# Splits of weights pinned in program order: the first of block 2 behind the experts' last copies, four of the feed-forward behind the layer norm

## The chip, the cores and the metric

One core of a Trainium2 chip. The metric is device time in microseconds (us) of one execution, as the median of several runs. The engines are PE (matrix products), ACT (ScalarE), DVE (VectorE), POOL (GpSimd) and SP (SyncE, which issues the DMAs here); each works through its own queue of instructions in order, and semaphores between them carry what one needs of another.

## The reference

Two blocks of a network, in fp32, for 256 tokens of width 1024. Block 1 is a mixer (attention and short convolution) and a mixture of experts; block 2 is a second mixer (attention and a gated MLP), a layer norm, a SwiGLU feed-forward of hidden width 2816, and a last layer norm:

```python
def first_block(x, ...):
    h = rms_norm(x, norm_mix_g[l])
    ...
    x = x + merged @ w_out[l]
    h2 = rms_norm(x, norm_ffn_g[l]).reshape(B * S, D)
    y = hierarchical_moe(h2, w_router_group[l], b_router_group[l], w_router_expert[l],
                         b_router_expert[l], w_gate_e[l], w_up_e[l], w_down_e[l])
    x = x + y.reshape(B, S, D)

def hierarchical_moe(...):
    for g in range(N_GROUPS):
        sl = slice(g * EXPERTS_PER_GROUP, (g + 1) * EXPERTS_PER_GROUP)
        act = jax.nn.silu(jnp.einsum('nd,edf->nef', h, w_gate[sl])) * jnp.einsum('nd,edf->nef', h, w_up[sl])
        act = act * combine[:, g, :, None]
        y = y + jnp.einsum('nef,efd->nd', act, w_down[sl])

def second_block(x, ...):
    mix = hybrid_mixer(x, w_in[l], ...)
    x = layer_norm(DEEPNORM_ALPHA * x + mix, ln1_g[l], ln1_b[l])
    ffn = swiglu_ffn(x, w_gate[l], w_up[l], w_down[l])
    x = layer_norm(DEEPNORM_ALPHA * x + ffn, ln2_g[l], ln2_b[l])

def swiglu_ffn(x, w_gate, w_up, w_down):
    return (jax.nn.silu(x @ w_gate) * (x @ w_up)) @ w_down
```

## The kernel before

All weights come from HBM as tiles of 128 x 2048 fp32 values (1 MB), which `Feed` loads through one ring of buffers: a buffer that is given back starts the DMA of the next tile in a fixed list, on SP's queue (L79). Products of weights with activations that need fp32 precision are made in three PE passes: each half tile of 128 x 1024 is split into a high part `whi` and a low part `wlo`, and the activations likewise (`xh` and `xl`). A **split** is two instructions, in `hi_lo` (L265 to 267): ACT copies the high part (L266), DVE subtracts it from the weight (L267). The class `Split` keeps the list of half tiles and makes splits ahead of their use: `ahead(n)` makes all up to the n-th, `get` hands one out and keeps `lead` splits in front of PE. Both write their instructions where the program calls them; under `manual_schedule` with `in_order` the engines keep the order of the program, but outside such a stretch, and where no instruction is tied down, a list scheduler sets the order of each engine.

The stages that matter here, in order of time:

- **The last expert group** (`group`, from L810). Eight rounds of gate and up products `pc_t<-w,xg` (L814), each followed by 12 small filler products on an otherwise idle bank (`warm`, L239), which use no result. Then `h = silu(gate) * up` on ACT and DVE (L843, L844), two transposes on PE (L848), the copy `hT` (L849), and the down products `pc_t<-w,hT` with four down tiles, their sums copied to `y` by ACT (L872, L867) and DVE, and PE's products of `y` with the scatter matrix (L854).
- **Block 2's first projection** (from L1108). `W.ahead(1)` splits the first half tile; then block 2's input, in `acc`, is made into high and low pieces of 256 columns (L266 and L267, the tile `x`), then come the second and the third split, and PE multiplies the pieces with the halves (L279).
- **The layer norm's stage** (from L1194). The end of the output projection is added to `xres` by DVE (L1180), with statistics (L1171 to 1176: `bst`, `mv`, `ve`), the reciprocal root `rs` on POOL (L257), the shift `mr` (L1197), the normalised rows `xn` on ACT (L1200), their transposes on PE (L1207), high and low pieces of them (`x`), and the first feed-forward products over two slices' gate and up weights together (L1237, L1240).
- **The feed-forward** (from L1268). 22 slices of 128 hidden columns. Slice f has a gate half and an up half (`fgu`), each multiplied with the pieces by `dense_wide` (L294, L295), whose two sums per bank DVE adds up (`gated`, L1272 to 1281: `fs`, `fu`), ACT applies silu to, DVE multiplies; `hi_lo` makes the slice's `fh` and `fl`. Every two slices the down projection's half tiles (`fdn`) are multiplied with these (L279, `pa_t<-whi,fh`). Each `W.get` in `hidden` asks for splits `lead` ahead; `W.lead` is set to 2 at the start of this stage and grows by one with each `get` (`W.grow`) up to the number of buffers.

Which split stands where, before: the scheduler sets block 2's first split on ACT and DVE ahead of `h` of the last group, and four splits of the feed-forward among DVE's and ACT's steps of the layer norm, as the listings below show.

Of the kernel before, what the change touches and what calls it, by code (L numbers as in the profile page):

```python
# [8 lines left out]
F32 = mybir.dt.float32  # L9
F32R = mybir.dt.float32r  # L10
I32 = mybir.dt.int32
BF16 = mybir.dt.bfloat16
AF = mybir.ActivationFunctionType
ALU = mybir.AluOpType
AX = mybir.AxisListType
PSUM = bass.MemoryType.PSUM

P = 128
D = 1024
KD = D // P  # L20
S = 256
# [13 lines left out]
WBUF = 3  # L35
WBUF2 = 9
# [90 lines left out]
def fused_blocks(ctx: ExitStack, tc: tile.TileContext, a, out):  # L127
# [4 lines left out]
    tt = nc.vector.tensor_tensor  # L132
    ts = nc.vector.tensor_scalar
    stt = nc.vector.scalar_tensor_tensor
    red = nc.vector.tensor_reduce
    act = nc.scalar.activation
# [7 lines left out]
    units_a, units_b, order = [], [], []  # L144
# [120 lines left out]
    def hi_lo(hi, lo, src):  # L265
        act(hi, src, AF.Copy)  # L266
        tt(out=lo, in0=src, in1=hi.bitcast(F32), op=ALU.subtract)  # L267

    def gained(hi, lo, src, g):
        act(hi, src, AF.Copy, scale=g)  # L270
# [664 lines left out]
    wes, wp = pool("w_b", bufs=WBUF2, side="left")  # L935
    xes, xp = pool("x_b", side="left")
    ees, ep = pool("blk2", side="right")
    W = Split(feed, wp, units_b, hi_lo, WBUF2, WBUF + 2)
    x_hl = xp.tile([P, 2, KD, S], F32R, name="x2")
    xh, xl = x_hl[:, 0], x_hl[:, 1]  # L940
    mh = xp.tile([P, KD, S], F32R, name="mh2")
# [164 lines left out]

    with tc.manual_schedule(engines=in_order):
        W.ahead(1)  # L1108
        for k in range(2):
            hi_lo(xh[:, k, :], xl[:, k, :], acc[0][:, k, :])  # L1110
        W.ahead(2)
        for k in range(2, KD, 2):
            hi_lo(xh[:, k:k + 2, :], xl[:, k:k + 2, :], acc[k // 2])
        W.ahead(3)
        for k in range(0, KD, 2):
            act(x2T[k // 4][:, k % 4:k % 4 + 2, :], acc[k // 2], AF.Copy)
        b2["z2"] = proj_tok(W, "z2", xh, xl, then([], [(x2_tok, 0, 0)], [(x2_tok, 0, 1)], [(x2_tok, 1, 0)]), bank_c)
# [68 lines left out]
    def scaled(o, t, cols, bias):  # L1186
        return stt(out=o, in0=xn[:, t, cols], scalar=ln[t][1], in1=bias[:, cols], op0=ALU.mult, op1=ALU.add)  # L1187

    tok = [slice(t * P, (t + 1) * P) for t in range(NT)]
    half = [slice(0, 512), slice(512, D)]  # L1190
    quarter = [slice(i * 256, (i + 1) * 256) for i in range(4)]
    with tc.manual_schedule(engines=in_order):
        for c in range(2):
            attn_rows(0, (3,), (c,))  # L1194
            stats(0, c, add_mix)
        shift = small(fp, 1, "mr")
        stt(out=shift, in0=ln[0][0], scalar=-1.0, in1=ln[0][1], op0=ALU.mult, op1=ALU.mult)  # L1197
        attn_rows(1, (0, 1), (0, 1))
        for cols in half:
            act(xn[:, 0, cols], xres[:, 0, cols], AF.Identity, scale=ln[0][1], bias=shift)  # L1200
        attn_rows(1, (2, 3), (0,))
        stats(1, 0, add_mix)

        def turned(src, t, k, z):

            for i in range(2):
                tr(z[:, k % 4 + i, :], src[:, t, (k + i) * P:(k + i + 1) * P], ident)  # L1207

        def in_chunks(z):
            return z.rearrange("p (k s) -> p k s", k=4)  # L1210

        z0 = [in_chunks(bank_c()) for _ in range(2)]
        for j in range(4):
            turned(xn, 0, 2 * j, z0[j // 2])
        attn_rows(1, (2, 3), (1,))
        ws = [[W.get("fgu", 4 + 2 * f + i) for i in range(2)] for f in range(2)]
        zs = [[two_parts(new()) for _ in range(2)] for new in (bank, bank_c)]

        def split3(t, j, src):
            ks = slice(2 * j, 2 * j + 2)  # L1220
            hi_lo(xh[:, ks, tok[t]], xl[:, ks, tok[t]], src)

        def part0(j):

            x3 = fp.tile([P, 2, P], F32, tag="x3", name="x3", bufs=2)
            for i in range(2):
                kc = 2 * j + i
                act(x3[:, i, :], z0[j // 2][:, kc % 4, :], AF.Identity, scale=V("ln1_g", kc), bias=V("ln1_b", kc))
            split3(0, j, x3)

        def first_hidden(t, j):

            for kc in (2 * j, 2 * j + 1):
                f = slice(kc * P, (kc + 1) * P)
                for w, z in zip(ws, zs):
                    for (hi, lo), z_ in zip(w, z):
                        mm(z_[:, :, tok[t]], hi[:, f], both(x_hl, kc, tok[t]), start=kc == 0 and t == 0, stop=False,  # L1237
                           skip_group_check=True)
                        if t:
                            mm(z_[:, 0, :], lo[:, f], xh[:, kc, :], start=False, stop=kc == KD - 1,  # L1240
                               skip_group_check=True)

        ln1 = feed.get("ln1")
        g1, b1 = ln1[:, 0:D], ln1[:, D:2 * D]
        part0(0)
        stats(1, 1, lambda t, c, o: (add_mix(t, c, o), part0(1)))
        part0(2)
        centred(1, half[0], g1)
        part0(3)
        for j in range(4):  # L1250
            first_hidden(0, j)
        z1 = [in_chunks(bank_c()) for _ in range(2)]

        def part1(j):
            scaled(xres[:, 1, quarter[j]], 1, quarter[j], b1)
            turned(xres, 1, 2 * j, z1[j // 2])

        part1(0)
        for j in range(4):
            if j < 3:  # L1260
                part1(j + 1)
            split3(1, j, z1[j // 2][:, 2 * (j % 2):2 * (j % 2) + 2, :])
            if j == 0:
                centred(1, half[1], g1)
            first_hidden(1, j)
        W.lead = 2


    acc = None
    held = {}  # L1270

    def gated(f, zg, zu):  # L1272
        s, u = [fp.tile([P, S], F32, tag=n, name=n, bufs=2) for n in ("fs", "fu")]
        red(out=s, in_=zg.rearrange("p b s -> p s b"), axis=AX.X, op=ALU.add)
        act(s, s, AF.Silu)
        red(out=u, in_=zu.rearrange("p b s -> p s b"), axis=AX.X, op=ALU.add)
        tt(out=s, in0=u, in1=s, op=ALU.mult)
        if f % 2 == 0:
            held[f // 2] = [fp.tile([P, 2, S], F32R, tag=n, name=n, bufs=2) for n in ("fh", "fl")]
        h_, l_ = held[f // 2]  # L1280
        hi_lo(h_[:, f % 2, :], l_[:, f % 2, :], s)

    def hidden(f):
        z = []
        for _ in range(2):
            z.append(two_parts(bank_c()))
            dense_wide(*W.get("fgu"), KD, x_hl, z[-1])
        gated(f, *z)

    for i in range(12):  # L1290
        if i < 11:
            for f in (2 * i, 2 * i + 1):
                if i:
                    hidden(f)
                else:
                    gated(f, *zs[f])
        if i in (1, 2):

            tc.keep_in_program_order(tt(out=xres[:, 0, :], in0=(xn if i == 1 else xres)[:, 0, :],
                                        in1=g1 if i == 1 else b1, op=ALU.mult if i == 1 else ALU.add))  # L1300
        if i == 2:
            feed.done(ln1)
        if 0 < i < 10:
            acc = acc or four_banks()
            rows_proj(W, "fdn", acc, *held.pop(i - 1), 0, i == 1, False)
# [110 lines left out]
```

## Time and profile before

| what | value |
|---|---|
| time, median of 3 runs | 708.74 us (708.24 to 709.82) |
| the profiled execution's own time | 707.57 us |
| its span in the profile | 705.8 us |
| mean clock granted to PE, share of full speed | 0.985 |
| PE busy | 656.4 us (93%) |
| DVE busy | 367.4 us (52%), of it 186.2 us in 151 low parts (L267) |
| ACT busy | 270.3 us (38%), of it 158.2 us in 151 high parts (L266) |
| POOL busy | 46.0 us (7%) |
| moved by DMA | 185.62 MB, mean 263 GB/s |

[...] In a timeline each row is a run of equal instructions on one engine: its start, the time from the start of the first to the end of the last, the line, the operation, and in brackets how long the engine was idle before and what released it. Neighbouring rows can overlap by some 0.1 us, since an instruction begins while the one ahead of it drains. A span of the profile is shorter than the time of the same execution, here by 1.77 us.

### The profile page before, as it was taken

Reading aid. Unit: us, or ns where it says so; the run is one execution under the profiler, and the core shown is the slowest. Engines: PE = TensorE matmul, PEld = TensorE weight load, DVE = VectorE, ACT = ScalarE, POOL = GpSimd, SP = SyncE. Lnnn points to the kernel's source line nnn. Section 1 sums busy time; section 2 is a strip of 40 time slices with the busy share of each in tenths; the row PEclk is TensorE's granted clock in tenths of the full one; section 3 lists DMA queues with packets and bytes.
Section 4 is the critical chain, followed back from the end, with each engine's and each line's share of the span. In section 5 each row is a group of like instructions: output and inputs, shape, how many; then the busy total and the mean of one; then the engine's idle time right before and its main releaser. Section 6 shows DMA issues by size and latency. Waiting matters only on the chain. (4 is left out here: it accounts for less than half of the span.)

```text
span 705.8 us, 10415 instructions
## 1 busy us (share of the span) xinstructions
PE 656.4 (93%) x4249; PEld 513.5 (73%) x4249; DVE 367.4 (52%) x578; ACT 270.3 (38%) x413; POOL 46.0 (7%) x60
## 2 busy tenths in 40 slices
PE   7999999999999898987787899999799999999995
PEld 6888999999955444434344588877588888888884
DVE  6667565555531202111000189867659766666646
ACT  6567644444300000000000295576535444444410
POOL 2222100000100000000000006101100000000001
PEclk9999999999999999999899799999999999999998
DMA  8983379738979999999999665742317755555001
GB/s 336 408 347 120 126 294 353 253 123 335 410 289 414 419 420 418 420 420 417 414 418 418 258 245 201 276 173 76 122 43 266 279 192 202 195 179 178 1 1 59
DMA packets 27558, 185.62 MB, mean 263 GB/s; under 512 B 3312, under 2 KB 3824, under 8 KB 5872
## 3 DMA queue, kind: packets, MB, share of 16 engines
q1 hardware_dynamic: 27504, 184.89, 67.5%
q8 instruction: 35, 0.57, 0.3%
q14 instruction: 19, 0.16, 0.1%
HBM read 183.83 MB, written 1.05 MB: 262 GB/s over the span
## 5 line engine op out<-in xcount | busy, mean ns | idle before, releaser
L267 DVE TENSOR_TENSOR wlo<-w,whi 128x1024 fp32r<-128x1024 f32 (+1 forms) x151 | 186.2, 1240 | 107.6 <-ACT whi L266 107.2
L266 ACT ACTIVATE whi<-w 128x1024 fp32r<-128x1024 f32 (+1 forms) x151 | 158.2, 1056 | 194.7 <-PE pa_t L279 59.8
L294 PE MATMUL pc_t<-x,whi 128*128 128x512 f32 x320 | 113.5, 399 | 0.0
L295 PE MATMUL pc_t<-x,wlo 128*128 128x256 f32 x320 | 89.8, 281 | 0.0
L294 PEld LDWEIGHTS pc_t<-x,whi 128*128 128x128 f32 x320 | 60.1, 188 | 14.8
L814 PE MATMUL pc_t<-w,xg 128*32 128x512 f32 x512 | 60.8, 615 | 5.0 <-PEq L886 5.0
L295 PEld LDWEIGHTS pc_t<-x,wlo 128*128 128x128 f32 x320 | 60.4, 189 | 0.4
L764 DVE TENSOR_TENSOR xg<-pc_t,vec 128x512 f32<-128x512 f32 (+2 forms) x18 | 11.4, 633 | 80.4 <-PE pc_t L763 80.4
L814 PEld LDWEIGHTS pc_t<-w,xg 128*32 128x32 f32 x512 | 15.5, 112 | 38.5 <-issue 34.8
L279 PE MATMUL pa_t<-whi,x 128*128 128x512 f32 x128 | 41.9, 397 | 0.0
L854 PEld LDWEIGHTS pa_t<-st,y 128*128 128x128 f32 x128 | 23.0, 189 | 21.9 <-DVE y L870 12.5
L854 PE MATMUL pa_t<-st,y 128*128 128x256 f32 x128 | 31.9, 392 | 6.3 <-DVE y L870 6.2
L814 PE MATMUL pc_t<-w,hT 128*32 128x512 f32 (+1 forms) x272 | 32.5, 593 | 4.1 <-ACT hT L849 4.1
L288 PE MATMUL pc_t<-xh,wlo 128*128 128x256 f32 x128 | 36.2, 283 | 0.0
L287 PE MATMUL pc_t<-xl,whi 128*128 128x256 f32 x128 | 36.2, 283 | 0.0
L286 PE MATMUL pc_t<-xh,whi 128*128 128x256 f32 x128 | 36.2, 283 | 0.0
L843 ACT ACTIVATE h<-pc_t 128x256 f32<-128x256 f32 x8 | 3.0, 381 | 86.2 <-PE pc_t L763 86.2
L763 PEld LDWEIGHTS pc_t<-pr,xres 128*128 128x128 f32 x256 | 29.3, 192 | 7.8 <-PE pc_t L814 4.2
L763 PE MATMUL pc_t<-pr,xres 128*128 128x128 f32 x256 | 31.1, 279 | 0.9 <-DVE pr L754 0.9
L870 DVE COPY y<-pc_t 128x512 f32<-128x512 f32 x7 | 4.8, 692 | 50.8 <-PE pc_t L814 50.8
L279 PE MATMUL pa_t<-whi,fh 128*128 128x512 f32 x88 | 28.7, 392 | 0.0
L279 PE MATMUL pa_t<-wlo,fh 128*128 128x512 f32 x88 | 28.6, 391 | 0.0
(313 smaller groups left out, 1220.8 us busy)
## 6 DMA issues: line engine op xcount, KB each, us to landing
w<-in_w_gu_dram SPq DMA_DIRECT2D x64, 1024.0 KB, 19.1
w<-in_w_dn_dram SPq DMA_DIRECT2D x32, 1024.0 KB, 19.4
w<-in_w_in_dram SPq DMA_DIRECT2D x28, 1024.0 KB, 12.6
w<-in_w_ffn_dram SPq DMA_DIRECT2D x22, 1024.0 KB, 4.9
w<-in_w_fdn_dram SPq DMA_DIRECT2D x11, 1024.0 KB, 4.9
w<-in_w_out_dram SPq DMA_DIRECT2D x8, 1024.0 KB, 4.9
w<-in_w_in_dram SPq DMA_DIRECT2D x4, 512.0 KB, 12.5
w<-in_w_cv_dram SPq DMA_DIRECT2D x2, 1024.0 KB, 9.2
```

Source lines behind the costliest of these rows:

```text
L266: act(hi, src, AF.Copy)
L267: tt(out=lo, in0=src, in1=hi.bitcast(F32), op=ALU.subtract)
L279: mm(acc[c], x_[:, kc, tok], w_[:, o + c * 512:o + (c + 1) * 512], start=first and i == 0 and n == 0, stop=last and i == len(ks) - 1 and n ...
L286: mm(acc, hi[:, f], xh[:, kc, :], start=kc == 0, stop=False)
L287: mm(acc, hi[:, f], xl[:, kc, :], start=False, stop=False)
L288: mm(acc, lo[:, f], xh[:, kc, :], start=False, stop=kc == nk - 1)
L294: mm(z, hi[:, f], x[:, :, kc, :], start=kc == 0, stop=False, skip_group_check=True)
L295: mm(z[:, 0, :], lo[:, f], x[:, 0, kc, :], start=False, stop=kc == nk - 1, skip_group_check=True)
L763: mm(zv[:, k, :], xres[:, t, kc * P:(kc + 1) * P], pr[:, t, :], start=t == 0, stop=t == 1)
L764: tt(out=xg[:, ks, :], in0=zv, in1=V("ffn_g")[:, ks].unsqueeze(2).to_broadcast([P, n, P]), op=ALU.mult)
L814: mm(out[sl, 0:n], x[:, sl], w[:, e * 512 + i * n:e * 512 + (i + 1) * n], start=start, stop=stop, skip_group_check=True)
L854: mm(acc[2 * c + k // 2][:, k % 2, :], ys[c][:, k * P:(k + 1) * P], st, start=False, stop=False, skip_group_check=True)
```

## The change

`hi_lo_here` is `hi_lo` with both instructions tied to their place in the program. `Split` starts with it, so that the first split of block 2 stands where `W.ahead(1)` is written, behind the copies of the last expert group; after that the usual `hi_lo` is back for the mixer. In the layer norm's stage the lead for the feed-forward is no longer asked for behind the first products; instead, at the stage's end, `W.ahead` and the first two slices' `gated` are written in alternation, inside the stretch in which the engines keep the program's order, and the splits of slices 2 to 4 that follow are tied down with `hi_lo_here` as well, up to slice 2's `hidden`. `W.lead` starts at 4 there instead of 2. `gated` itself is only moved up.

```diff
--- before.py
+++ after.py
@@ -265,6 +265,11 @@
     def hi_lo(hi, lo, src):
         act(hi, src, AF.Copy)
         tt(out=lo, in0=src, in1=hi.bitcast(F32), op=ALU.subtract)
+
+    def hi_lo_here(hi, lo, src):
+
+        tc.keep_in_program_order(act(hi, src, AF.Copy))
+        tc.keep_in_program_order(tt(out=lo, in0=src, in1=hi.bitcast(F32), op=ALU.subtract))
 
     def gained(hi, lo, src, g):
         act(hi, src, AF.Copy, scale=g)
@@ -935,7 +940,7 @@
     wes, wp = pool("w_b", bufs=WBUF2, side="left")
     xes, xp = pool("x_b", side="left")
     ees, ep = pool("blk2", side="right")
-    W = Split(feed, wp, units_b, hi_lo, WBUF2, WBUF + 2)
+    W = Split(feed, wp, units_b, hi_lo_here, WBUF2, WBUF + 2)
     x_hl = xp.tile([P, 2, KD, S], F32R, name="x2")
     xh, xl = x_hl[:, 0], x_hl[:, 1]
     mh = xp.tile([P, KD, S], F32R, name="mh2")
@@ -1106,6 +1111,7 @@
 
     with tc.manual_schedule(engines=in_order):
         W.ahead(1)
+        W.hi_lo = hi_lo
         for k in range(2):
             hi_lo(xh[:, k, :], xl[:, k, :], acc[0][:, k, :])
         W.ahead(2)
@@ -1186,6 +1192,19 @@
     def scaled(o, t, cols, bias):
         return stt(out=o, in0=xn[:, t, cols], scalar=ln[t][1], in1=bias[:, cols], op0=ALU.mult, op1=ALU.add)
 
+    held = {}
+
+    def gated(f, zg, zu):
+        s, u = [fp.tile([P, S], F32, tag=n, name=n, bufs=2) for n in ("fs", "fu")]
+        red(out=s, in_=zg.rearrange("p b s -> p s b"), axis=AX.X, op=ALU.add)
+        act(s, s, AF.Silu)
+        red(out=u, in_=zu.rearrange("p b s -> p s b"), axis=AX.X, op=ALU.add)
+        tt(out=s, in0=u, in1=s, op=ALU.mult)
+        if f % 2 == 0:
+            held[f // 2] = [fp.tile([P, 2, S], F32R, tag=n, name=n, bufs=2) for n in ("fh", "fl")]
+        h_, l_ = held[f // 2]
+        hi_lo(h_[:, f % 2, :], l_[:, f % 2, :], s)
+
     tok = [slice(t * P, (t + 1) * P) for t in range(NT)]
     half = [slice(0, 512), slice(512, D)]
     quarter = [slice(i * 256, (i + 1) * 256) for i in range(4)]
@@ -1263,22 +1282,15 @@
             if j == 0:
                 centred(1, half[1], g1)
             first_hidden(1, j)
-        W.lead = 2
+        W.ahead(W.n_got + 2)
+        for f in range(2):
+            gated(f, *zs[f])
+            W.ahead(W.n_got + 3 + f)
+    W.lead = 4
+    W.hi_lo = hi_lo_here
 
 
     acc = None
-    held = {}
-
-    def gated(f, zg, zu):
-        s, u = [fp.tile([P, S], F32, tag=n, name=n, bufs=2) for n in ("fs", "fu")]
-        red(out=s, in_=zg.rearrange("p b s -> p s b"), axis=AX.X, op=ALU.add)
-        act(s, s, AF.Silu)
-        red(out=u, in_=zu.rearrange("p b s -> p s b"), axis=AX.X, op=ALU.add)
-        tt(out=s, in0=u, in1=s, op=ALU.mult)
-        if f % 2 == 0:
-            held[f // 2] = [fp.tile([P, 2, S], F32R, tag=n, name=n, bufs=2) for n in ("fh", "fl")]
-        h_, l_ = held[f // 2]
-        hi_lo(h_[:, f % 2, :], l_[:, f % 2, :], s)
 
     def hidden(f):
         z = []
@@ -1289,11 +1301,10 @@
 
     for i in range(12):
         if i < 11:
-            for f in (2 * i, 2 * i + 1):
-                if i:
-                    hidden(f)
-                else:
-                    gated(f, *zs[f])
+            if i:
+                hidden(2 * i)
+                W.hi_lo = hi_lo
+                hidden(2 * i + 1)
         if i in (1, 2):
 
             tc.keep_in_program_order(tt(out=xres[:, 0, :], in0=(xn if i == 1 else xres)[:, 0, :],
```

How it moves instructions. First ACT at the end of the last expert group, before (`y`, `h` and `hT` are the group's copies; `whi` is block 2's first split; `x_5643` are the pieces of block 2's input):

```order
L872 ACTIVATE y<-pc_t 128x512
L266 ACTIVATE whi<-w 128x1024
L843 ACTIVATE h<-pc_t 128x256
L849 ACTIVATE hT<-pc_t 128x256
L872 ACTIVATE y<-pc_t 128x512
L867 ACTIVATE y<-pc_t 128x256
L266 ACTIVATE x_5643<-pa_t 128x256 x2
```

and now:

```order
L877 ACTIVATE y<-pc_t 128x512
L848 ACTIVATE h<-pc_t 128x256
L854 ACTIVATE hT<-pc_t 128x256
L877 ACTIVATE y<-pc_t 128x512
L872 ACTIVATE y<-pc_t 128x256
L271 ACTIVATE whi<-w 128x1024
L266 ACTIVATE x_5643<-pa_t 128x256 x2
```

The split has moved from ahead of `h` to behind the last copy of `y`, and stands right ahead of the two pieces of the input. DVE's half of it (`wlo`) has moved in the same way.

Second, DVE in the layer norm's stage, from the aggregated statistics `mv` of the first 128 tokens on, before (`ve` is the variance with its epsilon, `mr` the shift):

```order
L1174 BN_AGGR mv_6538<-bst 128x2
L267 TENSOR_TENSOR wlo<-w,whi 128x1024
L1176 TENSOR_SCALAR ve_6540<-mv_6538 128x1
L267 TENSOR_TENSOR wlo<-w,whi 128x1024
L1197 SCALAR_TENSOR_TENSOR mr_6544<-mv_6538,rs_37_6542 128x1
L1180 SCALAR_TENSOR_TENSOR xres<-pa_t,rs_34_6518,xres 128x512
L1171 BN_STATS bst<-xres 128x6
L267 TENSOR_TENSOR x_5643<-x_6589,x_5643 128x2x128
L1180 SCALAR_TENSOR_TENSOR xres<-pa_t,rs_34_6518,xres 128x512
L267 TENSOR_TENSOR wlo<-w,whi 128x1024
L267 TENSOR_TENSOR x_5643<-x_6595,x_5643 128x2x128
```

and now:

```order
L1180 BN_AGGR mv_6538<-bst 128x2
L1182 TENSOR_SCALAR ve_6540<-mv_6538 128x1
L1216 SCALAR_TENSOR_TENSOR mr_6544<-mv_6538,rs_37_6542 128x1
L1186 SCALAR_TENSOR_TENSOR xres<-pa_t,rs_34_6518,xres 128x512
L1177 BN_STATS bst<-xres 128x6
L267 TENSOR_TENSOR x_5643<-x_6589,x_5643 128x2x128
L1186 SCALAR_TENSOR_TENSOR xres<-pa_t,rs_34_6518,xres 128x512
L267 TENSOR_TENSOR x_5643<-x_6595,x_5643 128x2x128
L1177 BN_STATS bst<-xres 128x6
L1180 BN_AGGR mv_6601<-bst 128x2
```

The three `wlo` in these rows, and one more behind them, are gone from here.

Third, DVE at the start of the feed-forward, from slice 1's sums on (`fs` of the gate, `fu` of up; `fs<-fu,fs` is their product, `fl` its low part), before:

```order
L1274 TENSOR_REDUCE fs<-pc_t 128x256
L1276 TENSOR_REDUCE fu<-pc_t 128x256
L1277 TENSOR_TENSOR fs<-fu,fs 128x256 x2
L267 TENSOR_TENSOR wlo<-w,whi 128x1024
L267 TENSOR_TENSOR fl<-fs,fh 128x256 x2
L1274 TENSOR_REDUCE fs<-pc_t 128x256
L1276 TENSOR_REDUCE fu<-pc_t 128x256
L267 TENSOR_TENSOR wlo<-w,whi 128x1024
L1277 TENSOR_TENSOR fs<-fu,fs 128x256
L267 TENSOR_TENSOR wlo<-w,whi 128x1024
L267 TENSOR_TENSOR fl<-fs,fh 128x256
L267 TENSOR_TENSOR wlo<-w,whi 128x1024
```

and now:

```order
L1199 TENSOR_REDUCE fs<-pc_t 128x256
L1201 TENSOR_REDUCE fu<-pc_t 128x256
L1199 TENSOR_REDUCE fs<-pc_t 128x256
L1202 TENSOR_TENSOR fs<-fu,fs 128x256
L1201 TENSOR_REDUCE fu<-pc_t 128x256
L267 TENSOR_TENSOR fl<-fs,fh 128x256
L1202 TENSOR_TENSOR fs<-fu,fs 128x256
L1199 TENSOR_REDUCE fs<-pc_t 128x256
L267 TENSOR_TENSOR wlo<-w,whi 128x1024
L272 TENSOR_TENSOR wlo<-w,whi 128x1024 x3
L267 TENSOR_TENSOR fl<-fs,fh 128x256
L267 TENSOR_TENSOR wlo<-w,whi 128x1024 x4
```

The splits from slice 3's up half on now stand behind the sum of slice 3's own gate (the third `fs<-pc_t`, right ahead of them), and eight splits follow with one `fl` among them, where before single splits alternated with the sums. On PE the order changes at one place only: four products of the first down half (`pa_t<-whi,fh`) have moved into slice 3's up products. POOL's and SP's order is the same.

## Rows read from the trace of the kernel before

**Rows 1.** PE's waits from 376 to 706 us; us in total, times, longest.

```profile
PE pc_t L848 <- DVE h L844: 6.7, 1, 6.7
PE pa_t L1237 <- DVE x L267: 3.6, 3, 1.5
PE pc_t L1207 <- ACT xn L1200: 2.5, 1, 2.5
```

**Rows 2.** Timeline of ACT; start us, us, engine, operation, in brackets the idle time before.

```profile
387.81 1.06 ACT L266 ACTIVATE whi<-w 128x1024 fp32r<-128x1024 f32 x1 [30.21 <-DMA w<-in_w_in_dram]
388.77 0.37 ACT L843 ACTIVATE h<-pc_t 128x256 f32<-128x256 f32 x1
...
403.38 0.38 ACT L266 ACTIVATE x<-pa_t 128x256 fp32r<-128x256 f32 x1
404.33 0.38 ACT L266 ACTIVATE x<-pa_t 128x256 fp32r<-128x256 f32 x1 [0.57 <-DVE x L267]
```

**Rows 3.** Timeline of PE around the last expert group's first two stages.

```profile
381.17 1.06 PE L814 MATMUL pc_t<-w,xg 128*32 128x512 f32 x8
382.17 1.60 PE L239 MATMUL pc_t<-ident 128*128 128x128 f32 x12
390.51 0.69 PE L848 MATMUL pc_t<-ident,h 128*128 128x128 f32 x2 [6.74 <-DVE h L844]
391.73 1.94 PE L814 MATMUL pc_t<-w,hT 128*32 128x512 f32 x8 [0.53 <-ACT hT L849]
...
399.41 1.07 PE L814 MATMUL pc_t<-w,hT 128*32 128x256 f32 x16
...
405.18 0.58 PE L279 MATMUL pc_t<-whi,x 128*128 128x512 f32 x1
```

**Rows 4.** Timeline of DVE in the last expert group.

```profile
390.04 0.42 DVE L844 TENSOR_TENSOR h<-pc_t,h 128x256 f32<-128x256 f32 x1
```

**Rows 5.** Busy time by stretch: width, PE PEld DVE ACT POOL (instructions), PEclk, DMA, GB/s.

```profile
388.00:397.00 9.00, 5.96 (x26) 3.33 (x30) 1.56 (x2) 1.52 (x3) 1.10 (x1) 0.50 1.03 417
```

**Rows 6.** Timeline of DVE in the layer norm.

```profile
500.50 1.23 DVE L267 TENSOR_TENSOR wlo<-w,whi 128x1024 fp32r<-128x1024 f32 x1
501.65 0.15 DVE L1176 TENSOR_SCALAR ve<-mv 128x1 f32<-128x1 f32 x1
501.87 1.23 DVE L267 TENSOR_TENSOR wlo<-w,whi 128x1024 fp32r<-128x1024 f32 x1
503.53 0.16 DVE L1197 SCALAR_TENSOR_TENSOR mr<-mv,rs 128x1 f32<-128x1 f32 x1 [0.44 <-POOL rs L257]
```

**Rows 7.** Timeline of PE in the expert group before the last.

```profile
354.01 0.41 PE L848 MATMUL pc_t<-ident,h 128*128 128x128 f32 x2 [1.30 <-DVE h L844]
354.95 2.78 PE L814 MATMUL pc_t<-w,hT 128*32 128x512 f32 x24 [0.52 <-ACT hT L849]
```

**Rows 8.** SP's queue around the last group; DMA issues: KB each, us to landing.

```profile
358.66 8.23 SPq L79 DMA_DIRECT2D w<-in_w_dn_dram  x4
w<-in_w_dn_dram SPq DMA_DIRECT2D x4, 1024.0 KB, 19.9
```

**Rows 9.** Timeline of POOL in the layer norm.

```profile
497.23 0.55 POOL L257 TENSOR_TENSOR rs<-ms,mhalf 128x1 f32<-128x1 f32 x1 [0.36 <-DVE ms L262]
501.93 1.57 POOL L257 TENSOR_TENSOR rs<-ve,mhalf 128x1 f32<-128x1 f32 x1 [4.15 <-DVE ve L1176]
```

**Rows 10.** Busy time by stretch in the feed-forward, columns as in rows 5.

```profile
526.00:545.00 19.00, 19.00 (x103) 16.24 (x102) 18.78 (x26) 13.53 (x19) 0.00 (x0) 1.00 0.60 202
545.00:686.00 141.00, 141.00 (x743) 120.25 (x742) 94.45 (x118) 61.52 (x81) 0.00 (x0) 1.00 0.45 160
```

**Rows 11.** Timelines of DVE and PE in the feed-forward.

```profile
524.66 0.69 DVE L1274 TENSOR_REDUCE fs<-pa_t 128x256 f32<-128x512 f32 x1 [2.60 <-PE pa_t L1240]
...
531.05 1.22 DVE L267 TENSOR_TENSOR wlo<-w,whi 128x1024 fp32r<-128x1024 f32 x1
540.88 0.39 PE L294 MATMUL pc_t<-x,whi 128*128 128x512 f32 x1
```

## The prediction

> **What bounds the kernel now.** Start with the waits of the matmul engine from the middle of the run to its end [rows 1]: between 376 and 706 us PE waits in only three places for long: 6.7 us for `h` in the last expert group, 2.5 us for the normalised rows `xn`, and 3 times, 3.6 us together, for pieces of the layer norm's output. Elsewhere PE has work without a gap until the tail, so time removed there only helps if PE gets it. The change touches exactly these places and the feed-forward behind them.
>
> The 6.7 us first. ScalarE's rows [rows 2] show its cause: ScalarE sits idle 30.21 us until 387.81, when the DMA of block 2's first weights lands; it then splits that weight (1.06 us), and only behind it, at 388.77, comes `h`. The gate and up sums that `h` reads were done long before: PE's last weighted product of them starts at 381.17 (8 products, 1.06 us), followed by 12 filler products until 383.77 [rows 3]. So `h` was not waiting for its data but for its place in ScalarE's order. VectorE repeats it: a split's low half, then the product at 390.04 [rows 4]. PE resumes at 390.51.
>
> The idle costs twice. [...] Eight expert products take 1.94 us there [rows 3].
>
> In the layer norm the splits stand on the path itself [rows 6]: statistics end at 500.50, a split of 1.23 us follows, and the epsilon step that feeds the reciprocal root comes at 501.65; then another split, then the shift at 503.53.
>
> **The change, part by part. First place.** Ready at 382.3 (the last of the 8 products from 381.17), `h` takes 0.37 [rows 2] and VectorE's product 0.42 [rows 4]: `h` is whole at about 383.2, inside PE's filler. PE transposes it behind the filler, at 383.7 instead of 390.51. From there I price by full speed. In the group before, from the transposes to the first down product it is 0.94 [rows 7], so 384.6. Two rounds of 8 products and 12 fillers: from 381.17 to 383.70 such a round takes 2.53 [rows 3] (382.17 and 1.60, less the 0.07 by which rows overlap); two are 5.06, so the third down product stands at 389.7 instead of 399.41. From 399.41 to block 2's first product at 405.18 the clock was already full; this 5.77 stays: 395.45. **Gain 9.73 us**: 6.8 of wait, 2.9 of clock (7.68 against 5.06 between 391.73 and 399.41, and 1.22 against 0.94 before it).
>
> Can the weights follow? The four down tiles are issued from 358.66 over 8.23 us and land 19.9 us after issue [rows 8], the last by 386.8; PE wants them in order of arrival, from 384.6 on, the third at 389.7 and the fourth behind it. Block 2's first half is there at 387.8, wanted at 395. Neither is late by this count; the last down tile has 3 us in hand.
>
> What is late next: the split itself. ScalarE's last copy is now followed by the split's high half (1.06, [rows 2]), VectorE's by the low half (1.23, [rows 6]), and only then by the two pieces of block 2's input, which alternate between the two engines, each waiting for the other (0.57 at 404.33, [rows 2]). On the old clock of the trace: high half from 403.38 to 404.44, low half to 405.7, first piece whole at 406.05, second at 406.9. PE arrives at 405.18 and uses these in turn; its 12 products on them end about 0.75 late, and the next weight's low half follows 0.3 behind. Bounds: 0.5, and 2.3 if high and low half are paid in full. I take 1.0. **Net of the first place: -8.7 us.**
>
> **Second place.** Four splits leave the layer norm. The first, 500.50 to 501.73, held the epsilon step back 1.15 us: gain 1.15. The second does not delay a VectorE instruction by its own place, yet it stands beside the root on POOL: the root took 1.57 us there, and 0.55 in a row where VectorE was idle [rows 9]. I take 0.55, since VectorE has nothing to do until the root is there; then the shift comes at 501.35 instead of 503.53, 2.2 us earlier. The other end is 1.57, which gives 502.4.
>
> [...]
>
> Behind it the chain is short steps on three engines, whose lengths stay: the 2.2 us reach PE through its wait for `xn` (2.5 us, [rows 1]), whose data the shift makes. The third and fourth split stood between the pieces that PE waits for (the 3.6 us in 3 waits); with pieces of 0.42 and the products' spacing as before, I count 0.3, 0.1 and 0.9 for these waits, of which the last stays because it is a round trip between engines: 2.3 less. Summed, **a gain of 4.5 us**; 3.5 with the slow root.
>
> **Feed-forward.** The four splits have to be made somewhere: in the 19 us behind, VectorE is busy 18.78, in the rest of the feed-forward 94.45 of 141 [rows 10]. It was ahead of PE there by some 8 us: the first split of slice 4 starts at 531.05 and is done at 532.3, and PE comes to its product at 540.88 [rows 11]; 4 times 1.15 leaves over 3. So the store of splits pays, not PE, with one exception. In VectorE's new order the sum of slice 3's own gate stands ahead of the split of slice 3's up weight. PE must finish the gate, VectorE sum it (0.69, [rows 11]) and split (1.23), 1.9 in all, before PE's first low-half product. PE has one wide product and four products of the down projection to fill this, and these need the second of two high halves on ScalarE (1.06 each), which ScalarE reaches about 1.0 before the gate ends (counted on from VectorE's first sum at 524.66 by the durations above). That is 0.7 idle, then four products, then the low half. Bounds 0 and 1.9; I take 0.95. Later pairs stand as before. **Net of the second place: -3.55.**
>
> **Sum**: -8.7 - 3.55 = -12.25 us. The profiled execution has 707.57 (span 705.8, 1.77 around it), so 695.3; it lies 1.17 below the median of 708.74, and against that median the forecast is **696.5**.
>
> **Rivals.** (a) *The clock falls anyway.* PE still has a pause of about 0.5 us and light fillers. For: it fell in just this place. Against: in the group before, PE waits 1.30 and 0.52 us at the same steps [rows 7] at full speed. Price 2.9: 699.4. [...]
>
> (b) *The feed-forward takes back what the layer norm gave.* VectorE is full for 19 us and gets 4.6 us more; if PE had no store of splits, it would wait them out: 4.5 less 4.6, nothing left, 700.0. For: 18.78 of 19.0. Against: it was 8 us ahead.
>
> (c) *Slower: lockstep of sums and splits.* If the pinned order made each later slice wait as slice 3 does, a sum of its own gate ahead of its own up weight's split, 0.95 would be paid in up to 18 further slices, 17 us: 713.6. It turns the sign from 13 slices on (12.25 over 0.95). Against: the order shows it in slice 3 alone.
>
> **How the numbers follow.** Forecast 0.77, with a range of its own from 694.2 (stall of 0.5 at block 2, none in slice 3, the layer norm's third wait of 0.9 gone too: 2.35 less) to 698.8 (2.3 at block 2, slow root: 2.3 more); (a) 0.08, (b) 0.10, (c) 0.05. The range 694.2 to 699.7 holds the forecast's cases and (a), not (b) and (c). Faster by over 0.2% (1.4 us, about what a measurement of this kernel can tell from no change): 0.95, since (a) and (b) are faster too. The 0.05 of (c) is split: a lockstep in 12 to 14 slices would be within 0.2%, 0.02; in more, slower, 0.03.
>
> **What would show it.** Right: `h` at about 382.3 in the profile after; PE's wait for it gone and the clock at 1.00 from 383 to 400; block 2's first product near 395.5 with waits of about 1 us behind it; a root of about 0.55 us behind the first statistics; PE's three waits on `x` under 1 us each; one wait of about 0.7 at the first down-projection products. Wrong: if `h` still starts near 388, or PE waits repeatedly for `wlo` in the feed-forward.

## The result and the profile after

The changed kernel takes **698.89 us** (median of 4 runs, 697.34 to 700.64), the kernel before 709.13 (708.24 to 709.82): a ratio of 0.9849 with a 95% interval of 0.983 to 0.9868, or 10.2 us less. Forecast were 696.5 in a range of 694.2 to 699.7. The profiled execution took 697.34 us with a span of 695.6. It lies 1.55 us below its median and that of before 1.56 below its own, so the two spans may be set beside each other (705.8 less 695.6 is 10.2 too).

First the waits of PE from the middle of the run on (us in total, times, longest), which answer to [rows 1]:

```profile
PE pa_t L1256 <- DVE x L267: 1.3, 3, 0.9
PE pc_t L819 <- ACT hT L854: 0.5, 1, 0.5
PE pa_t L284 <- ACT whi L271: 0.4, 1, 0.4
PE pc_t L1226 <- ACT xn L1219: 0.4, 1, 0.4
```

The 6.7 us for `h` are gone; the wait for `xn` fell from 2.5 to 0.4, the three for pieces from 3.6 to 1.3, and one new wait has come, 0.4 for `whi` at L284. Now PE's timeline over the last expert group and the start of block 2, which answers to [rows 3]:

```profile
365.48 1.06 PE L819 MATMUL pc_t<-w,xg 128*32 128x512 f32 x8
...
384.19 1.60 PE L239 MATMUL pc_t<-ident 128*128 128x128 f32 x12
385.63 0.38 PE L853 MATMUL pc_t<-ident,h 128*128 128x128 f32 x2
386.55 1.07 PE L819 MATMUL pc_t<-w,hT 128*32 128x512 f32 x8 [0.53 <-ACT hT L854]
...
397.38 0.58 PE L284 MATMUL pc_t<-whi,x 128*128 128x512 f32 x1
...
403.92 0.60 PE L961 MATMUL pc_t<-ident,x2T 128*128 128x128 f32 x4
```

The last block of fillers starts at 384.19 (before: 382.17), and the transposes of `h` follow without a gap. Eight products take 1.07 us instead of 1.94: the granted clock stays at 1.00 from 366 to 400. From the last filler block to block 2's first product are 13.19 us where there were 23.01.

ScalarE and VectorE at the seam between the blocks, against [rows 2, 4]:

```profile
384.33 0.38 ACT L848 ACTIVATE h<-pc_t 128x256 f32<-128x256 f32 x1 [24.70 <-PE pc_t L819]
...
395.58 1.05 ACT L271 ACTIVATE whi<-w 128x1024 fp32r<-128x1024 f32 x1
396.53 0.38 ACT L266 ACTIVATE x<-pa_t 128x256 fp32r<-128x256 f32 x1
398.26 0.38 ACT L266 ACTIVATE x<-pa_t 128x256 fp32r<-128x256 f32 x1 [1.36 <-DVE x L267]
396.67 1.22 DVE L272 TENSOR_TENSOR wlo<-w,whi 128x1024 fp32r<-128x1024 f32 x1 [0.50 <-ACT whi L271]
397.81 0.42 DVE L267 TENSOR_TENSOR x<-pa_t,x 128x256 fp32r<-128x256 f32 x1
```

`h` starts when its sums are ready, at 384.33 and not at 388.77. The split (395.58 on ScalarE, 396.67 on VectorE) now stands in front of the pieces: the first is whole at 398.23, and ScalarE waits 1.36 for it before it can start the second. That is the stall with which block 2 begins.

The layer norm on VectorE and POOL, against [rows 6, 9]:

```profile
493.27 0.21 DVE L1180 BATCH_NORM_AGGREGATE mv<-bst 128x2 f32<-128x12 f32 x1
493.51 0.15 DVE L1182 TENSOR_SCALAR ve<-mv 128x1 f32<-128x1 f32 x1
494.38 0.16 DVE L1216 SCALAR_TENSOR_TENSOR mr<-mv,rs 128x1 f32<-128x1 f32 x1 [0.72 <-POOL rs L257]
493.80 0.55 POOL L257 TENSOR_TENSOR rs<-ve,mhalf 128x1 f32<-128x1 f32 x1 [3.05 <-DVE ve L1182]
```

From the end of the statistics (493.48) to the shift it is 0.90 us, where it was 3.03 (500.50 to 503.53); the root takes 0.55.

And the one new wait, in slice 3 of the feed-forward:

```profile
521.54 0.69 DVE L1199 TENSOR_REDUCE fs<-pc_t 128x256 f32<-128x512 f32 x1 [0.43 <-PE pc_t L300]
522.15 1.22 DVE L267 TENSOR_TENSOR wlo<-w,whi 128x1024 fp32r<-128x1024 f32 x1
522.26 1.19 PE L284 MATMUL pa_t<-whi,fh 128*128 128x512 f32 x4 [0.45 <-ACT whi L271]
523.42 0.39 PE L300 MATMUL pc_t<-x,wlo 128*128 128x256 f32 x1
```

VectorE sums slice 3's own gate at 521.54, splits the up weight behind it, and PE's first low-half product comes at 523.42. From slice 2's first product to slice 4's it is 22.03 us here (first two rows below), where the kernel before, with slice 2 at the third row, has 20.81 (its slice 4 starts at 540.88 [rows 11]):

```profile
508.62 0.48 PE L299 MATMUL pc_t<-x,whi 128*128 128x512 f32 x1
530.65 0.39 PE L299 MATMUL pc_t<-x,whi 128*128 128x512 f32 x1
520.07 0.48 PE L294 MATMUL pc_t<-x,whi 128*128 128x512 f32 x1
```

**Where the time went**, place by place, from the start of the same instruction of PE in both profiles:

| stretch of PE's work, up to | before, us | after, us | change | forecast |
|---|---|---|---|---|
| first product of the last expert group | 363.46 | 365.48 | **+2.02** | 0 |
| block 2's first product | 405.18 | 397.38 | -9.82 | -9.73 |
| first transposes of `x2T` | 410.82 | 403.92 | +0.90 | +1.0 |
| transposes of `xn` | 504.60 | 495.44 | -2.26 | -2.2 |
| first product of slice 2 | 520.07 | 508.62 | -2.29 | -2.3 |
| last `whi` product of slice 21 | 686.17 | 675.94 | +1.22 | +0.95 |
| sum | | | -10.23 | -12.28 |

Each change is the difference of the two columns less that of the line above. All terms of the forecast stand within 0.3 us; what is missing is in the first line, ahead of every instruction that the change moves. Of its 2.02 us, 0.46 are there before PE reaches the down products of the group before the last (355.41 against 354.95), and 1.56 come in 24 of these products, which take 4.34 us instead of 2.78.

### The profile page after: what moved, and what is told of

It reads as the page before. It is cut to its first block, busy times and chain, and to the rows that moved or that the text cites. A ratio compares the mean times of both kernels' runs of the same rounds, so it can differ in the third digit from the quotient of the medians.

```text
span 695.6 us, 10419 instructions
## 1 busy us (share of the span) xinstructions
PE 656.5 (94%) x4249; PEld 512.9 (74%) x4249; DVE 367.1 (53%) x578; ACT 270.2 (39%) x413; POOL 44.8 (6%) x60
## 5 line engine op out<-in xcount | busy, mean ns | idle before, releaser
L267 DVE TENSOR_TENSOR wlo<-w,whi 128x1024 fp32r<-128x1024 f32 (+1 forms) x147 | 180.9, 1239 | 79.0 <-ACT whi L266 78.9
L266 ACT ACTIVATE whi<-w 128x1024 fp32r<-128x1024 f32 (+1 forms) x147 | 153.7, 1056 | 151.6 <-PE pa_t L284 55.0
L284 PE MATMUL pa_t<-whi,x 128*128 128x512 f32 x128 | 41.9, 397 | 0.0
L284 PE MATMUL pa_t<-whi,fh 128*128 128x512 f32 x88 | 28.6, 394 | 0.4 <-ACT whi L271 0.4
L284 PE MATMUL pa_t<-wlo,fh 128*128 128x512 f32 x88 | 28.6, 392 | 0.0
```

The source lines that it names most:

```text
L284: mm(acc[c], x_[:, kc, tok], w_[:, o + c * 512:o + (c + 1) * 512], start=first and i == 0 and n == 0, stop=last and i == len(ks) - 1 and n ...
```

## Experiments

e1 and e3 are edits of the kernel before, all others of the changed kernel. Times are medians; the ratio is to the kernel before, run on the same chip.

| run | what | us | ratio, 95% interval |
|---|---|---|---|
| e1_first_only | first place alone | 702.40 | 0.9905, 0.9888 to 0.9921 |
| e2_second_only | second place alone | 705.44 | 0.9944, 0.9929 to 0.9959 |
| e3_fill | before, with fillers during the wait for `h` | 707.36 | 0.9979, 0.9967 to 0.9991 |
| e5_beside_root | changed, one low half back beside the root | 698.10 | 0.9839, 0.982 to 0.9859 |
| e6_between | changed, first split between the copies | 696.95 | 0.9826, 0.9807 to 0.9845 |
| e7_ffn_order | changed, other order in the feed-forward | 697.79 | 0.9843, 0.9821 to 0.9865 |
| e11_ffn_order2 | changed, the order of e7 with both sums of slice 2 tied | 696.72 | 0.9818, 0.98 to 0.9835 |
| e9_fill_g6 | changed, fillers in the group before the last | 696.74 | 0.983, 0.9809 to 0.985 |
| e10_all | e6, e7 and e9 together | 694.80 | 0.9801, 0.9783 to 0.982 |
| e12_all2 | e6, e11 and e9 together | 694.06 | 0.9795, 0.9776 to 0.9814 |

### Each place alone

e1 leaves the layer norm and the feed-forward as before, e2 leaves the first split as before. The edit of e1, from the kernel before:

```diff
-    W = Split(feed, wp, units_b, hi_lo, WBUF2, WBUF + 2)
+    W = Split(feed, wp, units_b, hi_lo_here, WBUF2, WBUF + 2)
...
         W.ahead(1)
+        W.hi_lo = hi_lo
```

and e2, from the changed kernel:

```diff
-    W = Split(feed, wp, units_b, hi_lo_here, WBUF2, WBUF + 2)
+    W = Split(feed, wp, units_b, hi_lo, WBUF2, WBUF + 2)
```

> Only the first place is changed: block 2's first split stands behind the experts' last copies, the layer norm and the feed-forward are as before. If the two places simply add up, this run is 8.7 to 8.9 us faster than before (about 700.3), PE's wait for h is gone, the clock is 1.00 from the last fillers to block 2, block 2 begins with about 0.9 us of waits, and the layer norm's waits (2.5 and 3.6 us) are unchanged. If part of the first gain depends on the second place, or if the stream of weights gives it back later, it is less than 8 us faster. If the change itself delays the stream of weights ahead of the last expert group (the 2 us that the changed kernel's profile lost there), the last group's first product starts about 2 us later than before here too; if that was chance, it starts within 1 us of before or scatters.

> Only the second place is changed: four splits leave the layer norm and the feed-forward is pinned; block 2's first split stands ahead of h as before. By the sum of its parts (4.4 gained in the layer norm, 1.2 lost in the feed-forward) it is 3.2 us faster than before, about 705.9, with the wait for h at 6 to 7 us, a root of 0.55 us on POOL, and one wait of about 0.45 for whi plus about 0.5 for wlo in slice 3. The rival that the feed-forward takes the layer norm's gain back expects no difference from before (709.1).

e1 is 0.95% faster, 6.5 us, not 8.7; e2 is 0.56% faster, 3.5 us, as worked out. The two add up to the whole: 0.95% and 0.56% are the changed kernel's 1.51%, each known to within 0.2%. So no trade between the two places shows, and what is missing belongs to the first place. Its own stretch gave what was forecast: in e1 block 2 begins 31.90 us behind the first product of the last group, as in the changed kernel, against 41.72 before. But the last group starts late in e1 too. The rows of the expert group before the last (PE), down to the first product of the last group, first in e1:

```profile
354.26 0.66 PE L853 MATMUL pc_t<-ident,h 128*128 128x128 f32 x2 [1.30 <-DVE h L849]
355.45 5.33 PE L819 MATMUL pc_t<-w,hT 128*32 128x512 f32 x24 [0.52 <-ACT hT L854]
...
366.50 1.06 PE L819 MATMUL pc_t<-w,xg 128*32 128x512 f32 x8
```

in e2, with block 2's first weight (ACT):

```profile
356.18 4.41 PE L819 MATMUL pc_t<-w,hT 128*32 128x512 f32 x24 [0.52 <-ACT hT L854]
...
366.34 1.07 PE L819 MATMUL pc_t<-w,xg 128*32 128x512 f32 x8
389.91 1.06 ACT L266 ACTIVATE whi<-w 128x1024 fp32r<-128x1024 f32 x1 [30.32 <-DMA w<-in_w_in_dram]
```

the same two places in e3, a run of the next section that also keeps the wait for `h`, and the last group's first product in the kernel before:

```profile
356.28 2.78 PE L814 MATMUL pc_t<-w,hT 128*32 128x512 f32 x24 [0.52 <-ACT hT L849]
389.73 1.06 ACT L266 ACTIVATE whi<-w 128x1024 fp32r<-128x1024 f32 x1 [30.81 <-DMA w<-in_w_in_dram]
363.46 1.07 PE L814 MATMUL pc_t<-w,xg 128*32 128x512 f32 x8
```

The 24 down products take 5.33 us in e1 and 4.41 in e2, 4.34 in the changed kernel, and 2.78 in e3 and in the kernel before [rows 7]. Their tiles are not late (the only idle time ahead of them is 0.52 us, for `hT`, in all five), it is the clock: from 352 to 362 the mean granted clock is 0.66 in e1, 0.83 in e2 and in the changed kernel, 1.00 in e3 and before. The changed kernel's stretches (width, PE, PEld, DVE, ACT, POOL busy, PEclk, which is the granted clock as a share of full speed, DMA share, GB/s):

```profile
352.00:356.00 4.00, 1.43 (x8) 0.60 (x12) 1.11 (x3) 1.04 (x3) 0.00 (x0) 0.90 1.01 418
356.00:358.00 2.00, 2.00 (x16) 0.42 (x12) 0.00 (x0) 0.00 (x0) 0.00 (x0) 0.50 1.01 418
```

PE was busy 1.43 of 4 us from 352 to 356, in the waits for `pg`, `h` and `hT`, and then the granted clock is at 0.50. e2 and e3 show why a kernel with the wait for `h` does not pay for this. In e2 the clock fell there (0.83), in e3 it held (1.00), and the last group starts at 366.34 and at 364.78, 1.56 apart. Block 2's first weight, for which `h` waits in both, lands at 389.91 and 389.73, only 0.18 apart: the transfers run without a break while PE is slow (DMA share 1.01 from 352 to 362 in both). Behind the wait for `h` such a loss was hidden; with the wait gone it reaches the end. That both weights land some 2 us later than in the profile of before (387.81 [rows 2]) is therefore not the clock's doing.

### The clock as a price of its own

e3 keeps the wait for `h` and fills it: 24 more filler calls behind the eighth round.

```diff
-                warm(lambda: idle, WARM2, ident)
+                warm(lambda: idle, WARM2 + (24 if kc == KD - 1 else 0), ident)
```

> The kernel before with 24 more filler calls (48 matmuls on the idle bank, about 6.1 us) behind the last round of gate and up products, so that PE is busy while it waits for h; the wait itself and all other orders stay. If the clock is a price of its own on top of the wait, it stays at 1.00 through the down products, and the run is 2.9 us faster than before (about 706.2) with h at its old place near 388. If the clock would fall in any case, or does not matter, the time is that of before. If fillers delay the transposes, it is up to 0.5 us slower than the first case.

The stretches of [rows 5] and of the layer norm in e3, and PE's rows:

```profile
388.00:397.00 9.00, 6.49 (x54) 4.27 (x52) 1.56 (x2) 1.71 (x3) 1.10 (x1) 1.00 1.03 416
505.00:510.00 5.00, 3.84 (x16) 3.06 (x14) 2.49 (x4) 4.49 (x10) 0.00 (x0) 0.73 0.01 5
392.44 0.44 PE L848 MATMUL pc_t<-ident,h 128*128 128x128 f32 x2 [1.98 <-DVE h L844]
...
404.24 0.58 PE L279 MATMUL pc_t<-whi,x 128*128 128x512 f32 x1
```

The clock is 1.00 from 388 to 397 instead of 0.50 [rows 5], and from the transposes of `h` to block 2's first product it is 11.80 us instead of 14.67: 2.87 less, the 2.9 that I had priced, with the wait untouched. The time fell by 1.6 us only (0.6 to 2.3 by the interval). In this execution the clock fell in the layer norm instead (0.73 from 505 to 510, where it was 1.00 before), behind the wait for `xn` (2.5 us before [rows 1]), and from the transposes of `xn` to slice 2 it took 1.43 us more than before. Whether that happened in the other runs no profile tells.

### Fillers where the clock falls

e9 puts fillers in three waits of the group before the last, on banks that are overwritten next.

```diff
+        warm(lambda: zs, fill, ident)
...
-            st_next = scatter(g + 1, pg)
+            st_next = scatter(g + 1, pg, 4 if g == NG - 2 else 0)
...
+        warm(lambda: za, 5 if g == NG - 2 else 0, ident)
...
+            warm(lambda: zy[0], 2 if g == NG - 2 and not c else 0, ident)
```

> The changed kernel with filler matmuls in three waits of PE in the expert group before the last (4 calls ahead of the scatter's transposes, 5 ahead of those of h, 2 ahead of the down products; 2.8 us together, where PE waits 1.1, 1.3 and 0.5). If the 2 us that the changed kernel loses ahead of the last group are the clock, which falls there in four of six profiles, the granted clock stays 1.00 from 350 to 365 us, the 24 down products take 2.8 us instead of 4.3 to 5.3, the last group starts 1.6 to 2.6 us earlier, and the median is 1.5 to 2.5 us less (by 698.9: about 696.9) with less scatter. If the loss is the stream of weights, the down products wait for their tiles instead and the time is the same. If the fillers get in the way, it is up to 0.5 us slower.

```profile
352.00:362.00 10.00, 9.53 (x71) 5.53 (x69) 1.45 (x3) 1.64 (x4) 0.00 (x0) 1.00 1.01 419
356.22 2.78 PE L820 MATMUL pc_t<-w,hT 128*32 128x512 f32 x24
```

The clock stays at 1.00, and the 24 products take 2.78. Over all profiles: without these fillers the clock fell there in 7 of 9 executions (the 24 products take 4.25 to 5.33 us), in the profile of before and in e3 it did not; with them (e9, e10, e12) in none of 3. The median is 2.1 us lower than the changed kernel's (1.3 by the two ratios to the kernel before); by the intervals alone (0.9809 to 0.985 against 0.983 to 0.9868) that would not be settled, the rows settle it for the place.

### The split in front of block 2

e6 ties the first split's high half behind the copy of the first down sum, its low half behind `h`'s product.

```diff
+                last["y"] = act(y, zy[0], AF.Copy)
...
+    def hi_lo_between(hi, lo, src):
+        for i, to in ((act(hi, src, AF.Copy), last["y"]),
+                      (tt(out=lo, in0=src, in1=hi.bitcast(F32), op=ALU.subtract), last["h"])):
+            tc.add_manual_dep(i.ins, to.ins.name, ...)
-    W = Split(feed, wp, units_b, hi_lo_here, WBUF2, WBUF + 2)
+    W = Split(feed, wp, units_b, hi_lo_between, WBUF2, WBUF + 2)
```

`last` holds the two instructions behind which the halves are tied, each noted where it is written (one shown).

> The changed kernel with block 2's first split tied not behind the last copies but between them: its high half behind the copy of the first down sum, its low half behind h's product, where both engines stand idle for 4 us and more. If the 0.9 us with which block 2 begins comes from the split in front of the first pieces, it goes: from block 2's first product to the transposes of x2T it is 5.6 us as in the kernel before, not 6.5, and the time is 0.9 us less than the changed kernel's (by 698.9: 698.0). If it comes from the alternation of the pieces between the two engines alone, 6.5 stays and so does the time. If the weight lands after the copy, the later copies are late and it is slower than the changed kernel.

```profile
398.72 0.58 PE L284 MATMUL pc_t<-whi,x 128*128 128x512 f32 x1
...
404.39 0.60 PE L969 MATMUL pc_t<-ident,x2T 128*128 128x128 f32 x4
397.80 0.38 ACT L266 ACTIVATE x<-pa_t 128x256 fp32r<-128x256 f32 x1 [0.50 <-DVE x L267]
```

From block 2's first product to `x2T` are 5.67 us, where the changed kernel has 6.54 and the kernel before 5.64: the stall is the split and not the alternation, whose wait is back at 0.50. The time is 1.9 us less than the changed kernel's (1.6 by the ratios); 0.87 of that is this place, the rest is not shown to be.

### The root on POOL

e5 puts one split back: its high half ahead of the last products of the first 128 tokens, its low half behind the epsilon step.

```diff
+        tc.keep_in_program_order(act(hi, part, AF.Copy))
         for c in range(2):
             attn_rows(0, (3,), (c,))
             stats(0, c, add_mix)
+        tc.keep_in_program_order(tt(out=lo, in0=part, in1=hi.bitcast(F32), op=ALU.subtract))
```

> The changed kernel with one split put back into the layer norm's stage: the high half ahead of the last products of the first 128 tokens, the low half right behind the epsilon step, where it runs while POOL makes the reciprocal root. If VectorE's subtraction from two tensors in SBUF holds the root up, the root takes about 1.57 us instead of 0.55 and ends about 0.4 us behind the low half; the shift comes 1.0 us later, PE's wait for xn grows by about 1.0, and the run is 0.5 to 1.2 us slower than the changed kernel, less what the feed-forward saves by one split. If the long root of the kernel before had another cause, it takes 0.55 and the time is that of the changed kernel.

```profile
494.29 0.15 DVE L1182 TENSOR_SCALAR ve<-mv 128x1 f32<-128x1 f32 x1
494.36 1.22 DVE L1221 TENSOR_TENSOR wlo<-w,whi 128x1024 fp32r<-128x1024 f32 x1
496.01 0.16 DVE L1229 SCALAR_TENSOR_TENSOR mr<-mv,rs 128x1 f32<-128x1 f32 x1 [0.44 <-POOL rs L257]
494.57 1.40 POOL L257 TENSOR_TENSOR rs<-ve,mhalf 128x1 f32<-128x1 f32 x1 [3.04 <-DVE ve L1182]
497.07 1.36 PE L1239 MATMUL pc_t<-ident,xn 128*128 128x128 f32 x8 [1.23 <-ACT xn L1232]
```

The root takes 1.40 us and ends at 495.97, 0.39 behind the low half; before it ended 0.40 behind its low half [rows 6, 9]. The shift comes 1.72 us behind the epsilon step instead of 0.87, and PE waits 1.23 for `xn` instead of 0.42. From `x2T` to the end this run is 0.95 us slower. Its median does not show it (698.10 against 698.89): a price of 1 us at one place is smaller than the scatter ahead of block 2, and only the rows tell it.

### The feed-forward's order

e7 makes the sums of slices 0 and 1 together and ties slice 2's gate sum behind the splits; e11 moves slice 3's up split ahead of the products as well and ties both sums of slice 2.

```diff
-        for f in range(2):
-            gated(f, *zs[f])
-            W.ahead(W.n_got + 3 + f)
+        sums = [summed(f, *zs[f]) for f in range(2)]
+        W.ahead(W.n_got + 3)
+        for f in range(2):
+            gated(f, *sums[f])
+        W.ahead(W.n_got + 4)
```

`summed` holds the two sums and the silu that `gated` held, and ties slice 2's gate sum to its place, in e11 its up sum too. e11 has, in place of the last four lines:

```diff
+        W.ahead(W.n_got + 4)
+        for f in range(2):
+            gated(f, *sums[f])
```

> The changed kernel with the first two slices' sums made together and the gate sum of slice 2 tied behind the splits, so that slice 3's up weight is split before the sums of slices 2 and 3. If PE's stall in slice 3 (0.45 for whi and 0.5 for wlo, 1.2 us in all) is the order of sums and splits, PE passes from slice 2 to slice 4 in the spacing of the other slices and the time is 1.0 to 1.2 us less than the changed kernel's (by 698.9: 697.8). If VectorE simply has too much to do there, the stall moves to another slice and the time is the same.

> The changed kernel with the first two slices' four sums first, then both splits of slice 3's weights, then the products of the first two slices, and both sums of slice 2 tied behind the splits that follow: no sum that waits for PE stands ahead of slice 3's split any more (in the try before, slice 2's up sum still did). If the stall of 1.2 us is this order, PE passes from slice 2 to slice 4 in 20.7 to 21.0 us as in the kernel before, instead of 21.95, with no wait for whi at the first down products, and the time is 1.0 us less than the changed kernel's, less or more by the scatter of about 1 us ahead of block 2. If four more splits are too much for VectorE there, PE still waits for wlo or whi in slices 3 to 5 and the passage stays near 21.9.

e7 missed. Another sum had come to stand in the way (VectorE, then PE; the last two rows are PE in e11):

```profile
519.24 0.69 DVE L1203 TENSOR_REDUCE fu<-pc_t 128x256 f32<-128x512 f32 x1 [0.43 <-PE pc_t L300]
520.18 0.42 DVE L1209 TENSOR_TENSOR fs<-fu,fs 128x256 f32<-128x256 f32 x1
523.00 0.73 PE L284 MATMUL pa_t<-whi,fh 128*128 128x512 f32 x2 [0.44 <-ACT whi L271]
510.20 0.48 PE L299 MATMUL pc_t<-x,whi 128*128 128x512 f32 x1
531.02 0.39 PE L299 MATMUL pc_t<-x,whi 128*128 128x512 f32 x1
```

Slice 2's up sum at 519.24 waits for PE, and slice 1's product (520.18), its `fh` on ScalarE and the next high half all stand behind it; PE waits 0.44 for `whi`, as in the changed kernel, and takes 21.78 us from slice 2 to slice 4 where that takes 22.03. The median came out as expected all the same, 1.1 us lower: by these rows 0.25 of it is this place, and nothing shows the rest to be the edit's, so that hit was luck. In e11 no such sum is left, and from slice 2's first product to slice 4's it is 20.82 us, as in the kernel before (20.81) and not 22.03 as in the changed one. The stall was order, not load.

### Together

> The three edits together: the split between the copies, the feed-forward's sums behind the splits, the fillers in the group before the last. If the three places are in a row on PE's path and none hands its gain to the next, their gains add: 0.9, 1.1 and 2.0, about 4 us less than the changed kernel (694.9 by 698.9). If the stream of weights takes over once PE is faster, less: block 2's second weight is landed near 389 and its third near 391, and PE's last group cannot pass its last down tile, which lands near 387.

> This order of the feed-forward with the two other edits (the first split between the copies, fillers in the group before the last). If the gains add, it is 0.8 to 1.0 us less than the run of all three edits before (694.8), about 693.9, and 15 us less than before. If another wait takes the place of the stall, 694.8 stays.

e10 has the edits of e6, e7 and e9, e12 those of e6, e11 and e9. e12 takes 694.06 us, 2.05% less than the kernel before, and its interval (0.9776 to 0.9814) lies clear below the changed kernel's (0.983 to 0.9868): it beats both. Of PE's waits from 376 us on, that for `whi` is gone:

```profile
PE pa_t L1276 <- DVE x L267: 1.2, 2, 0.9
PE pc_t L820 <- ACT hT L858: 0.5, 1, 0.5
PE pc_t L1246 <- ACT xn L1239: 0.4, 1, 0.4
```

e10 took 694.80, almost the 694.9 expected, though one of its three gains failed to come: with e7's order PE still takes 21.82 us from slice 2 to slice 4. In part that hit is luck. e12 takes 20.82 there.

## Why the prediction was right, and where it was off

**First place, -8.7.** The mechanism was right in each step: `h` waited for its place in ScalarE's order, the clock was a second price (0.50 from 388 to 397 before [rows 5], 1.00 in e3, which gave 2.87 of the 2.9), and the split became the next late thing (0.90 of 1.0, shown by e6). The gain of 9.73 (9.71 by its own terms) came out as 9.82. The step that was off is "From there I price by full speed" together with what I read from the group before: "PE waits 1.30 and 0.52 us at the same steps at full speed" [rows 7]. That was one execution, and one of the two in nine in which the clock held there. In the other seven it fell behind the same waits, and the 24 products took 4.25 to 5.33 us instead of 2.78, 1.5 to 2.6 more. I took the 6.8 us of waiting as all gain, when part of it had been a cover for whatever made PE late ahead of it: in the profile after, 2.02 us, of which 1.56 is the clock. Rival (a) had the mechanism, in the wrong group and at 2.9 us. And that 698.89 lies inside the range is in part luck: the forecast's own cases end at 698.8, and only the price of (a) takes the range to 699.7.

The instructions of PE up to this place do not settle the clock: in nine executions with the same ones its mean from 352 to 362 was 0.66 to 0.83 in seven and 1.00 in two.

**Second place, -3.55.** The median of e2 gives -3.5, the rows -2.26, -2.29 and +1.22, together -3.33. That the root would be 0.55 and not 1.57 held, and e5 shows the low half to be the cause. The row from which I took the 0.55 was misread, though: beside the root at 497.23 VectorE was idle for 0.17 us only and then, from 497.40, added sums out of PSUM to `xres` (0.75 us). The root at 496.32, with VectorE idle throughout, took 0.55 too. The stall in slice 3 was mis-sized, 1.22 us against my 0.95; e11 shows that all of it was the order. Rival (b) fell: VectorE's store was enough, since the same splits cost nothing in e11. Rival (c) fell too: behind slice 3 the distance between the two kernels' products stays at 10.23 us from slice 4 to the end.

**What stays open.** Why the clock held in two of nine executions, and whether seven in nine holds beyond the profiles: e5's profiled execution has a mean granted clock of 0.986, its other three have 0.992 and 0.993 and are 0.5 to 1.2 us shorter. How much of the remaining 2.4 us between forecast and median is the clock alone: seven losses and two zeros are 1.4 us on average, and what e9 gave is uncertain by about 2 us. The time at which the weights land also differs between executions (387.81 in the profile of before [rows 2], 389.91 in e2, 389.73 in e3), with the same products on PE up to there but for e3's fillers.

## What to carry to other kernels

A wait that ends on a transfer can hide delays ahead of it: here 1.6 us of slow products did not show behind a wait of 6 us, since they did not hold the transfer up. Before its length is counted as gain, ask how late the engine may come in a bad run, not in the one profile at hand; what comes before the wait is on the path once it is gone. And when splits or copies are moved behind a stage, look at which sums or reductions stand ahead of them: here one that waited for the matmul engine held up all that stood behind it (22.03 us from slice 2 to slice 4, 20.82 with both sums tied behind the splits), and the cure was its place, not less work.

## What I had not expected of the hardware

The clock fell behind waits that looked harmless: 1.1, 1.3 and 0.5 us, PE busy 1.43 us of 352 to 356, and then 0.50 from 356 to 358. With some 2.9 us of filler products in these waits it was 1.00 from 352 to 362 in three of three profiles.

Where VectorE was in an instruction on two tensors in SBUF when POOL's root began, the root ended 0.39 to 0.42 us behind the end of that instruction, as if it waited it out. It made no difference whether VectorE had 1.0 to 1.2 us still to go (the low halves in the kernel before and in e5) or 0.25 (the piece beside the second root of the changed kernel, 500.28 to 500.69, root from 500.44 to 501.10). The changed kernel's root at 683.92, beside VectorE's `xn` from 683.75 to 685.02, took 1.52. The other way round no row shows a wait: VectorE's product `z`, begun 0.25 us behind the changed kernel's root at 450.57 (0.56 us), took 0.69, as did the one at 448.80 with no root beside it.
